# First stage of a hybrid encoder step: TensorE's queue written down in slots of one channel tile

## The chip, the cores and the metric

One core of a Trainium2 chip runs the whole step in one launch. The metric is the device time of that launch in microseconds; runs of one kernel are compared by their median. Engines are named as the profile names them: PE is TensorE, DVE is VectorE, ACT is ScalarE, POOL is GpSimd, and SP is SyncE, which issues every DMA of this kernel.

## What is computed

One layer takes 4096 tokens of a new stream (the prompt) and 32 tokens of a running one (the sample), 1024 wide:

```python
h    = rmsnorm(x, ln_pre)
proj = h @ w_in            # B_a | C_a | X_a | Z_a | qkv | Z_g | a_dec | b_beta
# group A: y_a = B_a * conv3(C_a * X_a) * silu(Z_a)                  (512 channels)
# group B: q, k, v = silu(conv4(qkv)); q, k L2-normalised            (4 heads of 128)
a_mat = strict_lower((kb * beta) @ kb.T) * decay
t_mat = triangular_solve(a_mat, eye, unit_diagonal=True)
u, w  = t_mat @ (v * beta), t_mat @ (k * beta * exp(g))
# chunk after chunk, with the state S handed on:
v_new = u - w @ S
o     = (q * exp(g)) @ S + attn @ v_new
S     = S * exp(g_last) + kdec.T @ v_new
y = x + rmsnorm(concat(y_a, rmsnorm(o) * silu(Z_g)) @ w_out, ln_post)
```

Each product of the big matrices is made of three products of float16 halves; the small products of group B are float32.

## The kernel before, in words

The program has two stages. **The first stage** makes group B: it projects q, k, v and Z_g and runs the gated recurrence. **The second stage** makes group A and the output product. Only the first is touched.

The prompt is cut into 16 blocks of 256 tokens, each with two chunks of 128 tokens. A block has 16 channel tiles of 128 columns of `w_in`, which `proj` takes in pairs: `qkv_pair` for k (two pairs), q (two) and v (two), `z_pair` for Z_g (two). One channel tile is 8 x 3 = 24 matmuls of 128x256 (lines 388 to 390, tiles `pj..`). The table `steps` (line 746) names the eight pairs in their order. Behind a pair, ACT copies the bank into `u`, ACT and DVE run the convolution (lines 403 and 405), and ACT the silu.

The rest of a block's group B is a chain of small groups of PE instructions with DVE, ACT or POOL work between them:

- `stage1(b, c)`, for each chunk: four transposes of k and of q (line 426, tile `gt`), then the gram products of k with k and q (line 442, `gq`), which DVE multiplies with the decay into `M` and `at` (lines 443 and 444).
- `subst(b)`: the 32x32 diagonal blocks of `M` go out to `lad` (line 450) and come back as `la` (line 485); DVE makes a factor `rl` (lines 488 to 490); POOL then runs a forward substitution, one multiply (line 495) and 31 pairs of a multiply and a subtract (lines 499 and 500), each waiting for the one before. The result goes out to `ltd` (line 503) and comes back in eight small DMAs as `Tc` (line 510).
- `merge(b)`: five groups of small PE instructions (lines 546, 551, 554, 557 and 560, tile `m`), with DVE or ACT between any two of them, build the inverse `U` out of `Tc` and `M`. DVE transposes `Tc` into `U` (line 531).
- `rec_a(b, c)`: transposes of v (`rt`), products with the state S (`rk`, `rq`, lines 580 and 585), with `U` (`rv`, line 591) and the update of S (`rS`, line 596). `rec_b(b, c)`: the product with `at` (`oo`), a norm on DVE and ACT, transposes (`om`, line 625) and the gate.

Around these stand `xprep` of the next block (norm of x, transposes by DMA), `gates` and `decays` of the next block (the tiles `ggate`, `gcs`, `gB`), and `prep_a`, which prepares the second stage's weights in 16 halves on DVE, ACT and POOL.

The main loop (line 767) runs over groups: group 0 holds the sample and block 0, group 1 block 1, and so on. Inside a group it emits the eight pairs, and between them the small groups: `finish(prevs, si)` for the block before in steps 0 to 3, `stage1` of this block in steps 4 and 5 (3 and 4 in the last `LS` = 2 groups). That is the order in which the code is written, not the order on the engines. The program is built with `schedule_with_timeline_sim=True`: a scheduler with its own costs of every instruction decides the order of each engine's queue, and on PE it places the small groups, often in pieces, between single matmuls of a channel tile. On the chip each engine works through its queue in that order and waits on semaphores.

PSUM tiles come from `bank`: `pj`, `g` and `r` have two buffers each, `o` and `m` one.

Of the kernel before, what the change touches and what calls it, by code (L numbers as in the profile page):

```python
# [18 lines left out]
P = 128  # L19
# [15 lines left out]
LS = 2  # L35
# [15 lines left out]
def hybrid_kernel(  # L51
# [7 lines left out]
    V, G, A, T = nc.vector, nc.gpsimd, nc.scalar, nc.tensor  # L59
# [107 lines left out]

    def scaled(cts, n=P, urow=None):


        ws = []
        first = cts[0] >= 16
        nm = f"{cts[0]}"
        L = bank("r" if first else "g", [P, 2, P], f"L{nm}")[:, :len(cts), :n]
        for i, ct in enumerate(cts):
# [10 lines left out]
            if not first:  # L186
                for kn in (4, 2, 1):
                    V.tensor_tensor(ab[:, 0:kn], ab[:, 0:kn], ab[:, kn:2 * kn], ALU.add)
            for k in range(kn):
                T.matmul(L[:, i], ones16, ab[:, k, :], start=k == 0, stop=k == kn - 1)  # L190
            ws.append(w)
        e = te([P, 2, P], I32, "we", 1, nm)[:, :len(cts), :n]
# [8 lines left out]
        for i, w in enumerate(ws):  # L201
            V.tensor_tensor(w, w, bc(e[:, i].bitcast(F32), 1, KT), ALU.mult)
        if urow is None:
# [4 lines left out]
        return ws  # L208
# [173 lines left out]
    def proj(b, cts, nm):  # L382
        n = b["n"]
        pt = bank("pj", [P, 2, NB1], f"{b['id']}_{nm}")
        for i, ct in enumerate(cts):
            wh, wl = W[ct]
            for k in range(KT):
                T.matmul(pt[:, i, :n], wh[:, k, :], b["hi"][:, k, :n], start=k == 0, stop=False)  # L388
                T.matmul(pt[:, i, :n], wh[:, k, :], b["lo"][:, k, :n], start=False, stop=False)  # L389
                T.matmul(pt[:, i, :n], wl[:, k, :], b["hi"][:, k, :n], start=False, stop=k == KT - 1)  # L390
        return pt

    def qkv_pair(b, c0, dst):

        n = b["n"]
        pt = proj(b, (16 + c0, 17 + c0), f"c{c0}")
# [11 lines left out]
    def z_pair(b, c0):  # L408
        n = b["n"]
        pt = proj(b, (28 + c0, 29 + c0), f"z{c0}")  # L410
# [4 lines left out]
    def stage1(b, c):  # L415
# [4 lines left out]
        ss = b["ss"]  # L420
        nm = f"{b['id']}_{c}"
        jk = te([P, P], BF16, "jk", 2, nm)
        for x in range(2):
            tp = bank("g", [P, NH, P], f"t{x}{nm}")
            for h in range(NH):
                T.transpose(tp[:C, h, :], qk[:, h, x, sl], ident)
            for h in range(NH):
                A.activation(jk[:C], tp[:C, h, :], AF.Square, accum_out=ss[:, c, x, h:h + 1])
            if x == 0:
                kd = (te if b["s"] else tl)([P, NH, P], F32, "hl" if b["s"] else "kd", 4, nm)[:C]  # L430
                V.tensor_tensor(kd, tp[:C], bc(b["ed"][:, c], 2, P), ALU.mult)
                b["kd"].append(kd)
# [15 lines left out]
        for q in range(C // 32):  # L448
            s = slice(32 * q, 32 * q + 32)
            dma(b["lad"][c, :, q].rearrange("h j i -> j h i"), M[s, :, s])  # L450

# [64 lines left out]
    def merge(b):  # L516
# [26 lines left out]
        for q in (0, 2):  # L543
# [3 lines left out]
            V.tensor_tensor(X[s1], px[s1], bc(nb_[s1], 3, 32), ALU.mult)  # L547
        for q in (0, 2):
# [3 lines left out]
            A.activation(U[s0, :, :, s1], pu[s0], AF.Copy)  # L552
        for c, h in ch:
            T.transpose(pt[:, c, h], U[0:64, c, h, 0:64], ident[:64, :64])
        A.activation(Y[0:64], pt, AF.Copy)
        for c, h in ch:
            T.matmul(py[:, c, h], M[c][0:64, h, 64:128], Y[0:64, c, h], start=True, stop=True)
        V.tensor_tensor(Y[64:128], py, bc(nb_[64:128], 3, 64), ALU.mult)
        for c, h in ch:
# [5 lines left out]
    def rec_a(b, c):  # L565
# [4 lines left out]
        qk, v, U, kd = b["qk"], b["v"], b["U"][c], b["kd"][c]  # L570
        S = state[b["s"]]
# [4 lines left out]
        for h in range(NH):  # L576
            A.activation(R[:, h], vt[:, h], AF.Copy, scale=b["br"][:, c, h:h + 1])
        pk = bank("r", [P, NH, P], f"k{nm}")[:C]
# [8 lines left out]
        for h in range(NH):  # L587
            A.activation(o[:, h], pq[:, h], AF.Copy, scale=b["e1"][:, c, h:h + 1])
        pv = bank("r", [P, NH, P], f"v{nm}")[:C]
# [3 lines left out]
        A.activation(vn, pv, AF.Copy)  # L593
        pS = bank("r", [P, NH, P], f"S{nm}")
# [6 lines left out]
        b["rec"] = (o, vn)  # L601

    def rec_b(b, c):
# [4 lines left out]
        o, vn = b["rec"]  # L608
# [13 lines left out]
        V.tensor_tensor(o, o, bc(f, 2, P), ALU.mult)  # L622
        pm = bank("o", [P, NH, P], f"m{nm}")[:, :, :C]
# [10 lines left out]
    def setup_block(b):  # L634
# [10 lines left out]
        b["kd"], b["M"], b["at"] = [], [], []  # L645

    def prep_b(ct):

        for i, w in enumerate(scaled((ct, ct + 1))):
# [6 lines left out]

    wa = {"next": 0}

    def prep_a():
# [7 lines left out]
        if not half:  # L667
            wa["w"] = scaled((ct, ct + 1))
# [70 lines left out]
    wgf, = scaled((32,), 8, ug)  # L739
# [8 lines left out]
    def finish(prevs, si):  # L748

        for p in prevs:  # L750
            n = p["nch"]
            if si == 0:
                merge(p)
            elif si == 1:
                rec_a(p, 0)
            elif si == 2:
                rec_b(p, 0)
                if n > 1:
                    rec_a(p, 1)
            elif si == 3:  # L760
                if n > 1:
                    rec_b(p, 1)
                if p["last"]:
                    out_state(p)

    prevs = []
    for gi, grp in enumerate(groups):
        for b in grp:
            setup_block(b)
            if b["s"]:  # L770
                b["hist"] = te([P, 12, 3], F32, "hists", 2, "i")
                if gi:
                    for c in range(0, 12, 2):
                        init_hist(b, 16 + c)
                state[1] = te([P, NH, P], F32, "hl", 4, "s0")
                dma(state[1], state_gdn[0, 0].rearrange("h k v -> k h v"))
            elif gi:
                b["hist"] = groups[gi - 1][-1]["hist_new"]
        for si, (kind, c0) in enumerate(steps):
            if gi == 0 and si == 4:  # L780
# [3 lines left out]
            if gi == 0:  # L784
                for kd_, c_ in steps[:si + 1 + (AH if si >= AS else 0)]:
                    ct = (28 if kd_ == "z" else 16) + c_
                    if ct not in W:
                        prep_b(ct)
                if kind != "z":
                    init_hist(smp, 16 + c0)  # L790
            for b in grp:
                n = b["n"]
                if kind == "z":
                    z_pair(b, c0)
                elif kind == "v":
                    qkv_pair(b, c0, b["v"][:, c0 - 8:c0 - 6, :n])
                else:
                    h0 = c0 % 4
                    qkv_pair(b, c0, b["qk"][:, h0:h0 + 2, 0 if kind == "k" else 1, :n])
            finish(prevs, si)  # L800
            if si == (2 if gi else 6) and gi + 1 < len(groups):
                for b in groups[gi + 1]:
                    xprep(b)
            s1 = 4 if gi + LS < len(groups) else 3
            if si in (s1, s1 + 1):
                for b in grp:
                    if si - s1 < b["nch"]:
                        stage1(b, si - s1)
            if si == s1 + 1:
# [3 lines left out]
            if si == (3 if gi else 7) and gi + 1 < len(groups):  # L813
                in_turn([gates(b) for b in groups[gi + 1]])
            if si == 6 and 1 <= gi <= 13 or si == 2 and gi in (4, 7, 10):

                p = grp[-1] if si == 6 else prevs[-1]
# [435 lines left out]
```

## Time and profile before

| | |
|---|---|
| Runs | 2394.66 us median of 3 (2390.61 to 2403.79) |
| The profiled execution | 2393.51 us, span 2391.8 us |
| PE busy | 2156.4 us, 90% of the span |
| PE weight loads | 1706.8 us, 71% |
| DVE busy | 1699.0 us, 71% |
| ACT busy | 992.5 us, 41% |
| POOL busy | 1195.2 us, 50% |
| Mean granted clock of PE | 0.962 |

The profiled execution lies 1.15 us below the median of the runs. The first stage reaches from the start to about 1320 us, the second from there to the end, with the recurrence of the last two blocks beside its beginning. The busy time of PE counts modelled ends of pipelined matmuls that overlap, so the distance from start to start is what a matmul costs. A number behind "<-" in a row names what ended an idle time of the engine.

### The profile page before, as it was taken

How to read it: one execution, taken by the hardware profiler on the slowest of the kernel's cores; microseconds unless marked ns; L12 is line 12 of the kernel's file. 1: busy time of each engine (PE TensorE's matmuls, PEld its weight loads, DVE VectorE, ACT ScalarE, POOL GpSimd, SP SyncE). 2: the span in 40 equal slices, each digit the busy share in tenths (PEclk: the TensorE clock that was granted, in tenths of full speed). 3: DMA queues.
4: the chain of work that ended last, by engine and by line, in shares of the span. 5: the costliest groups of instructions: out<-in, count | busy, mean ns of one | idle time of the engine just before them, and what ended most of it. 6: DMA issues, size and time to landing. Idle time of an engine off the chain costs nothing. (4 is left out here: it accounts for less than half of the span.)

```text
span 2391.8 us, 48652 instructions
## 1 busy us (share of the span) xinstructions
PE 2156.4 (90%) x18626; PEld 1706.8 (71%) x18626; DVE 1699.0 (71%) x4666; ACT 992.5 (41%) x2497; POOL 1195.2 (50%) x1581
## 2 busy tenths in 40 slices
PE   3677989899999999999999799899999999999998
PEld 3566877778777777787778678788888887444443
DVE  4886878987689888786777675676575565666763
ACT  4454656565666566555654220222121121433321
POOL 3526246752575644454454740766456611554542
PEclk9888999999999999999989899999999999999999
DMA  6334333534333442244324304311211133443431
GB/s 117 53 93 106 80 75 96 116 82 92 92 100 78 109 112 75 68 91 118 70 72 125 101 24 174 104 66 54 80 59 39 54 100 98 136 150 115 157 115 54
DMA packets 296913, 221.39 MB, mean 93 GB/s; under 512 B 166392, under 2 KB 236856, under 8 KB 296680
## 3 DMA queue, kind: packets, MB, share of 16 engines
q1 hardware_dynamic: 296680, 218.28, 33.5%
q8 instruction: 146, 2.39, 0.4%
q14 instruction: 87, 0.71, 0.1%
HBM read 127.84 MB, written 74.64 MB: 85 GB/s over the span
## 5 line engine op out<-in xcount | busy, mean ns | idle before, releaser
L388 PE MATMUL pj_c<-hhi,w 128*128 128x256 f16 x1536 | 429.3, 280 | 1.2 <-DMA hhi<-xth 1.2
L390 PE MATMUL pj_c<-hhi,w 128*128 128x256 f16 x1536 | 429.7, 280 | 0.0
L389 PE MATMUL pj_c<-hlo,w 128*128 128x256 f16 x1536 | 428.9, 279 | 0.0
L867 PEld LDWEIGHTS <-w_a 128*128 128x128 f16 x2880 | 269.9, 99 | 59.5 <-issue 25.6
L1130 PEld LDWEIGHTS <-opm 128*128 128x128 f16 x1536 | 149.6, 98 | 189.8 <-issue 15.5
L500 POOL TENSOR_TENSOR lt<-lt 128x112 f32<-128x112 f32 (+29 forms) x496 | 250.0, 504 | 38.9
L495 POOL TENSOR_TENSOR la<-la,lt 128x1024 f32<-128x1024 f32 x16 | 38.7, 2421 | 449.9 <-DVE lt L490 270.9
L390 PEld LDWEIGHTS <-w 128*128 128x128 f16 x2176 | 215.5, 100 | 53.2 <-POOL w L652 23.0
L499 POOL TENSOR_TENSOR lt<-la,lt 128x112 f32<-128x112 f32 (+29 forms) x496 | 233.1, 470 | 38.8
L388 PEld LDWEIGHTS <-w 128*128 128x128 f16 x2176 | 215.8, 100 | 34.1 <-issue 2.1
L389 PEld LDWEIGHTS <-w 128*128 128x128 f16 x2176 | 215.7, 100 | 30.7 <-issue 0.5
L405 DVE SCALAR_TENSOR_TENSOR qk<-u,cw,qk 128x256 f32<-128x256 f32 x384 | 214.9, 596 | 9.0 <-ACT qk L403 8.4
L867 PE MATMUL pja<-op,w_a 128*128 128x256 f16 x1536 | 194.5, 276 | 7.0 <-DVE w L881 3.4
L1079 POOL TENSOR_TENSOR mab<-mab 128x1024 bf16<-128x1024 bf16 (+2 forms) x48 | 103.6, 2159 | 130.8 <-ACT mab L1077 128.4
L867 PE MATMUL ga<-op,w_a 128*128 128x256 f16 x1152 | 149.8, 275 | 14.0 <-DVE w L881 8.1
L389 PE MATMUL pj_z<-hlo,w 128*128 128x256 f16 x512 | 144.6, 282 | 0.0
L390 PE MATMUL pj_z<-hhi,w 128*128 128x256 f16 x512 | 144.4, 282 | 0.0
L388 PE MATMUL pj_z<-hhi,w 128*128 128x256 f16 x512 | 144.3, 282 | 0.0
L1130 PE MATMUL pjo<-w_o,opm 128*128 128x512 f16 x528 | 118.2, 379 | 3.8 <-DVE v13y L1154 2.0
L1130 PE MATMUL ro<-w_o,opm 128*128 128x512 f16 x504 | 114.7, 383 | 3.9 <-DVE v7y L1154 2.0
L881 DVE TENSOR_TENSOR w<-pja,w 128x256 f32<-128x256 f32 x168 | 67.4, 420 | 70.6 <-PE pja L867 68.0
L1130 PE MATMUL go<-w_o,opm 128*128 128x512 f16 x504 | 112.7, 379 | 3.9 <-DVE v19y L1154 2.0
(707 smaller groups left out, 4946.5 us busy)
## 6 DMA issues: line engine op xcount, KB each, us to landing
xt<-in_x_prompt_dram SPq DMA_DIRECT2D x32, 512.0 KB
op<-hTd SPq DMA_DIRECT2D x32, 512.0 KB
mx<-mxd SPq DMA_DIRECT2D x16, 1024.0 KB
xtw<-in_w_in_dram SPq DMA_DIRECT2D x28, 512.0 KB
wad<-hl SPq DMA_DIRECT2D x56, 256.0 KB
gB<-gd SPq DMA_DIRECT2D x16, 516.0 KB
hTd<-hhi SPq DMA_DIRECT2D x16, 512.0 KB
hTd<-hlo SPq DMA_DIRECT2D x16, 512.0 KB
```

What stands on the lines that cost most here:

```text
L388: T.matmul(pt[:, i, :n], wh[:, k, :], b["hi"][:, k, :n], start=k == 0, stop=False)
L389: T.matmul(pt[:, i, :n], wh[:, k, :], b["lo"][:, k, :n], start=False, stop=False)
L390: T.matmul(pt[:, i, :n], wl[:, k, :], b["hi"][:, k, :n], start=False, stop=k == KT - 1)
L405: V.scalar_tensor_tensor(d, u[:, i, j:j + n], cw[:, j, c0 + i:c0 + i + 1], d, ALU.mult, ALU.add)
L495: E.tensor_tensor(la, la, bc(rl, 1, 32), ALU.mult)
L499: E.tensor_tensor(tm, bc(la[:, j, j + 1:32], 2, w), bc(lt[:, j, 0:w], 1, r), ALU.mult)
L500: last = E.tensor_tensor(lt[:, j + 1:32, 0:w], lt[:, j + 1:32, 0:w], tm, ALU.subtract)
L867: T.matmul(out, lt(x, k), rh(y, k), start=start and k == n == 0, stop=stop and k == 3 and n == 2)
L881: V.tensor_tensor(dst, p, src, ALU.add)
L1079: G.tensor_tensor(ab[:, 0:m], ab[:, 0:m], ab[:, m:2 * m], ALU.add)
L1130: T.matmul(p, mo[:, x, k, t * P:t * P + m], WO[y, k][:, hf * 512:hf * 512 + 512], start=k == i == 0, stop=k == KT - 1 and i == 2)
```

## The change

PE's order in the first stage no longer comes from the scheduler. A wrapper `Ordered` stands in for `nc.tensor`: from group 1 to the end of the first stage it ties every PE instruction to the one written before it, without a semaphore. The other engines' queues are still made by the scheduler, around that fixed order.

The code is therefore written in the order that PE is to have. The unit is a slot, one channel tile of 24 matmuls; a block has 16 of them, and slot number s0 + i is the i-th one from the start of block b's own group (s0 = 16 x group). `at_slot` files a function under a slot, `run_slot` calls the functions of a slot behind its channel tile. The functions with PE work in several parts became generators (`qkv_pair`, `z_pair`, `merge`, `rec_a`, `rec_b`, `scaled`, `prep_a`), so that each part can be filed by itself; `stage1` is split into `norm_qk` and `gram`. `LS` is gone: the last blocks are treated as the others. In `scaled`, for the second stage's weights, the last of three additions writes to a tile of its own and the bank `L` is taken later.

```diff
-    V, G, A, T = nc.vector, nc.gpsimd, nc.scalar, nc.tensor
+    V, G, A = nc.vector, nc.gpsimd, nc.scalar
+    class Ordered:
+        on = False
+        last = None
+        def queue(self, i):
+            ins = getattr(i, "ins", i)
+            if self.on and self.last is not None:
+                tc.add_manual_dep(ins, self.last.name, mybir.DependencyInfo(
+                    mybir.DependencyClass.NoSync, mybir.DependencyReason.DATA), reason="order")
+            self.last = ins
+            return i
...
+    T = Ordered()
...
-    def finish(prevs, si):
...
+    def finish(p, s0):
...
+        at_slot(s0 + 22, next, ra[0])
+        at_slot(s0 + 23, next, ra[0])
+        for i in range(5):
+            at_slot(s0 + 24 + i, next, mg, None)
+        at_slot(s0 + 29, next, ra[0])
+        at_slot(s0 + 30, ends, ra[0])
+        at_slot(s0 + 30, next, rb[0])
+        at_slot(s0 + 28, next, ra[1])
+        at_slot(s0 + 32, next, ra[1])
+        at_slot(s0 + 34, next, ra[1])
+        at_slot(s0 + 34, ends, rb[0])
+        at_slot(s0 + 35, ends, ra[1])
+        at_slot(s0 + 35, next, rb[1])
+        at_slot(s0 + 39, ends, rb[1])
...
+            T.on = True
...
+            at_slot(s0 + 7, norm_qk, b, 0, 0)
+            at_slot(s0 + 8, norm_qk, b, 1, 0)
+            at_slot(s0 + 10, norm_qk, b, 0, 1)
+            at_slot(s0 + 11, gram, b, 0)
+            at_slot(s0 + 11, norm_qk, b, 1, 1)
+            at_slot(s0 + 12, gram, b, 1)
+            at_slot(s0 + 12, rnorms, b)
+            at_slot(s0 + 12, subst, b)
+            if gi + 1 < len(groups):
+                nx = groups[gi + 1][0]
+                g = gates(nx)
+                at_slot(s0 + 2, xprep, nx)
+                at_slot(s0 + 9, next, g)
+                at_slot(s0 + 10, next, g)
+                at_slot(s0 + 13, ends, g)
+            finish(b, s0)
+            for si, (kind, c0) in enumerate(steps):
+                ps = pair(b, kind, c0)
+                next(ps)
+                run_slot(s0 + 2 * si)
+                ends(ps)
+                run_slot(s0 + 2 * si + 1)
...
+                        with tc.issue_after(p["subst_end"]):
+                            pa = prep_a()
+                            if next(pa, 0) is None:
+                                at_slot(s0 + 11, next, pa)
+                                at_slot(s0 + 13, ends, pa)
...
+    T.on = False
```

Two places in the built order show what moves. The first is PE where the merge of block 8 begins, during the channel tiles of block 9. `pj9_..` is a bank of that block's projection, `m8` the merge's bank, `Tc8` the substitution's result. Before:

```order
L388 LDWEIGHTS w20_26_1454
L388 MATMUL pj9_c10_11530<-hhi9_10167,w20_26_1454 128x256
L546 MATMUL m8_10906<-Tc8_10676,M8_0_10462 32x32
L389 LDWEIGHTS w20_26_1454
L389 MATMUL pj9_c10_11530<-hlo9_10168,w20_26_1454 128x256
L546 MATMUL m8_10906<-Tc8_10676,M8_0_10462 32x32
L390 LDWEIGHTS w21_26_1455
L390 MATMUL pj9_c10_11530<-hhi9_10167,w21_26_1455 128x256
```

With the change (the wrapper's lines 74 and 77 stand for all matmuls and transposes):

```order
L74 LDWEIGHTS w17_24_1209
L74 MATMUL pj9_c8_11197<-hhi9_9848,w17_24_1209 128x256
L74 MATMUL m8_11227<-Tc8_10596,M8_0_10411 32x32 x4
L74 MATMUL m8_11227<-Tc8_10596,M8_1_10481 32x32 x4
L74 MATMUL m8_11227<-Tc8_10596,M8_0_10411 32x32 x4
L74 MATMUL m8_11227<-Tc8_10596,M8_1_10481 32x32 x4
L77 MATMUL gt09_1_11247<-ident_63,qk9_10776 128x128 x4
L74 LDWEIGHTS w18_25_1212
```

The merge's first group was spread over the matmuls of a channel tile, one piece between a few of them; it now stands in one piece behind the tile of slot 8.

The second place is DVE where it takes up `Tc7`, the substitution's result of block 7 (`o6`, `zg6`: the output of block 6; `kd8`, `u8`, `v8`: stage 1 and convolution of block 8; `u9`: of block 9). Before:

```order
L621 TENSOR_TENSOR so6_1_9217<-so6_1_9217,sm6_8457 128x4
L398 COPY u9_6_11019<-hist8_9784 128x2x3
L531 STREAM_TRANSPOSE U_144<-Tc7_9625 32x8x32 x2
L622 TENSOR_TENSOR o6_1_9062<-o6_1_9062,so6_1_9217 128x512
L531 STREAM_TRANSPOSE U_144<-Tc7_9625 32x8x32 x2
L547 TENSOR_TENSOR Rx7_9853<-m7_9854,sm7_9540 32x256
L431 TENSOR_TENSOR kd8_1_10550<-gt08_1_10541,E38_9313 128x512
```

With the change:

```order
L471 TENSOR_TENSOR kd8_0_10124<-gt08_0_10115,E38_9602 128x512
L429 COPY u8_10_10389<-hist7_8640 128x2x3
L583 STREAM_TRANSPOSE U_144<-Tc7_9538 32x8x32 x4
L599 TENSOR_TENSOR Rx7_10187<-m7_10188,sm7_9453 32x256 x2
L471 TENSOR_TENSOR kd8_1_10217<-gt08_1_10208,E38_9602 128x512
L431 COPY hist8_9725<-u8_8_10243 128x6
L436 SCALAR_TENSOR_TENSOR v8_9723<-u8_8_10243,cw_98,v8_9723 128x256 x3
```

Before, block 7's `Tc` was taken up after the next block's first gram and beside the output of block 6; now before that gram, with the convolution of v of block 8 behind it in the queue.

## Rows read from the trace of the kernel before

**Rows 1.** Busy time by engine in one stretch, with granted clock and DMA:

```profile
core 0: us, PE busy (x) PEld busy (x) DVE busy (x) ACT busy (x) POOL busy (x), PEclk, DMA share, GB/s
300.00:1300.00 1000.00, 923.16 (x8568) 782.44 (x8569) 798.60 (x2442) 576.97 (x1570) 548.67 (x1019) 0.96 0.38 91
```

**Rows 2.** Waits of PE, 444 to 1055 us (total us, times, longest):

```profile
PE m L546 <- DMA Tc<-ltd: 12.7, 9, 2.4
PE rk L580 <- DVE S L599: 8.2, 8, 3.0
```

**Rows 3.** PE in time (start, length, [idle before]): merges of blocks 0, 8, 9, 10, 15:

```profile
241.66 0.24 PE L546 MATMUL m<-Tc,M 32*32 32x32 f32 x2
...
830.78 0.24 PE L546 MATMUL m<-Tc,M 32*32 32x32 f32 x2 [1.43 <-DMA Tc<-ltd]
...
911.32 0.24 PE L546 MATMUL m<-Tc,M 32*32 32x32 f32 x2 [1.98 <-DMA Tc<-ltd]
...
991.64 0.24 PE L546 MATMUL m<-Tc,M 32*32 32x32 f32 x2 [1.75 <-DMA Tc<-ltd]
...
1370.91 0.31 PE L546 MATMUL m<-Tc,M 32*32 32x32 f32 x2 [6.09 <-DMA Tc<-ltd]
```

**Rows 4.** PE in order of time: last gram products of blocks 9 and 10:

```profile
857.70 1.03 PE L442 MATMUL gq<-qk 128*128 128x256 f32 x4
...
939.03 1.03 PE L442 MATMUL gq<-qk 128*128 128x256 f32 x4
```

**Rows 5.** Block 9 from gram to merge: DVE, SP and POOL in order of time:

```profile
858.76 0.42 DVE L443 TENSOR_TENSOR M<-gq,gB 128x256 f32<-128x256 f32 x1
...
859.22 1.73 SPq L450 DMA_DIRECT2D lad<-M  x4
...
863.73 1.71 SPq L485 DMA_DIRECT2D la<-lad  x4
...
867.81 0.19 DVE L488 TENSOR_SCALAR lt<-la 128x32 f32<-128x32 f32 x1 [0.76 <-DMA la<-lad]
...
868.69 2.36 POOL L495 TENSOR_TENSOR la<-la,lt 128x1024 f32<-128x1024 f32 x1 [23.74 <-DVE xss L115]
...
907.34 0.20 POOL L500 TENSOR_TENSOR lt<-lt 128x8 f32<-128x8 f32 x1
...
909.30 4.28 SPq L510 DMA_DIRECT2D Tc<-ltd  x8
```

**Rows 6.** PE in order of time: what groups cost from start to start:

```profile
707.28 1.16 PE L585 MATMUL rq<-S,qk 128*128 128x128 f32 x8
708.28 1.03 PE L442 MATMUL gq<-qk 128*128 128x256 f32 x4
709.24 0.69 PE L551 MATMUL m<-U,Rx 32*32 32x32 f32 x16
709.86 0.28 PE L388 MATMUL pj_c<-hhi,w 128*128 128x256 f16 x1
...
712.38 1.03 PE L442 MATMUL gq<-qk 128*128 128x256 f32 x4
```

**Rows 7.** Busy time and granted clock behind one merge:

```profile
911.70:921.90 10.20, 9.52 (x51) 5.76 (x51) 10.16 (x20) 4.28 (x12) 8.66 (x11) 0.50 0.37 87
```

**Rows 8.** PE in order of time: the last projection matmul of the first stage:

```profile
1320.27 0.27 PE L390 MATMUL pj_z<-hhi,w 128*128 128x256 f16 x1
```

**Rows 9.** DVE by line, 444 to 1055 us (busy, mean ns); four steps at 915.86:

```profile
L405 DVE SCALAR_TENSOR_TENSOR v<-u,cw,v 128x256 f32<-128x256 f32 x96 | 46.1, 517 | 0.9 <-ACT v L403 0.6
...
L531 DVE STREAM_TRANSPOSE U<-Tc 32x256 f32<-32x256 f32 x32 | 13.9, 435 | 13.1 <-DMA gd<-row 6.7 <-DMA Tc<-ltd 6.0
...
915.86 4.59 DVE L405 SCALAR_TENSOR_TENSOR v<-u,cw,v 128x256 f32<-128x256 f32 x4
```

**Rows 10.** Busy time during the substitutions of blocks 9 and 13:

```profile
868.70:907.50 38.80, 34.27 (x326) 30.60 (x325) 35.44 (x97) 22.45 (x54) 33.94 (x63) 1.00 0.50 103
1187.60:1221.20 33.60, 33.60 (x330) 30.94 (x328) 28.01 (x77) 16.91 (x59) 28.74 (x64) 1.00 0.13 43
```

More of the change, by code (lines that the diff above doesn't have):

```diff
@@ L202, in scaled @@
             V.tensor_tensor(w, w, bc(e[:, i].bitcast(F32), 1, KT), ALU.mult)
+        if not first:
+            yield
         if urow is None:
@@ L667, in prep_a @@
         if not half:
-            wa["w"] = scaled((ct, ct + 1))
+            yield from scaled((ct, ct + 1))
             return
@@ L746, in hybrid_kernel, with at_slot, run_slot, ends @@
     steps = [("k", 4), ("k", 6), ("q", 0), ("q", 2), ("v", 8), ("v", 10), ("z", 0), ("z", 2)]
-    def finish(prevs, si):
[L750 to L767, printed above, removed]
+    slots = {}
+    def at_slot(i, fn, *a):
+        slots.setdefault(i, []).append(lambda: fn(*a))
+    def run_slot(i):
+        for fn in slots.pop(i, ()):
+            fn()
+    def ends(gen):
+        for _ in gen:
+            pass
+    def finish(p, s0):
+        n = p["nch"]
+        ra = [rec_a(p, c) for c in range(n)]
+        rb = [rec_b(p, c) for c in range(n)]
+        mg = merge(p)
+        if n == 1:
+            for i, g in enumerate((ra[0], ra[0], mg, ra[0], ra[0], rb[0])):
+                at_slot(s0 + 16 + i, next, g, None)
+            at_slot(s0 + 24, ends, rb[0])
+            at_slot(s0 + 24, out_state, p)
+            return
+        at_slot(s0 + 22, next, ra[0])
[12 more added lines that the diff above has]
+        at_slot(s0 + 39, ends, rb[1])
+        if p["last"]:
+            at_slot(s0 + 36, out_state, p)
+    def first_group(grp):
         for b in grp:
@@ L783, in hybrid_kernel @@
                     decays(b)
[L784 to L790, printed above, removed]
-            for b in grp:
[L792 to L805, printed above, removed]
+            for kd_, c_ in steps[:si + 1 + (AH if si >= AS else 0)]:
+                ct = (28 if kd_ == "z" else 16) + c_
+                if ct not in W:
+                    prep_b(ct)
+            if kind != "z":
+                init_hist(smp, 16 + c0)
+            for b in grp:
+                ends(pair(b, kind, c0))
+            if si == 6:
+                xprep(groups[1][0])
+            if si in (4, 5):
                 for b in grp:
-                    if si - s1 < b["nch"]:
-                        stage1(b, si - s1)
-            if si == s1 + 1:
+                    if si - 4 < b["nch"]:
+                        stage1(b, si - 4)
+            if si == 5:
                 for b in grp:
@@ L826, in hybrid_kernel @@
         prevs = grp
-    while wa["next"] < 16:
-        prep_a()
+    T.on = False
     early.close()
-    for si in range(4):
-        finish(prevs, si)
+    for i in sorted(slots):
+        run_slot(i)
     late.close()
```

149 lines of the change are left out of this document (95 added, 54 removed).

## The prediction

> **What bounds the kernel now.** I read the table of stretches first. From 300 to 1300 us PE is busy 923 of 1000 us, DVE 799, POOL 549, at a mean clock of 0.96 [rows 1]: PE seems to be the bound of the first stage, with little idle time. The waits of PE come next. Over eight blocks the longest is for `Tc`, the substitution's result (12.7 us), then for the state S (8.2) [rows 2]. A queue written by hand could win those few microseconds per block. But which waits are left depends on what PE's queue may put in front of the substitution, so the third view is a block's loop, in order of time.
>
> The merge of block 0 begins at 241.66 us, that of block 15 at 1370.91 [rows 3]: 1129.25 us for 15 blocks, **75.3 us a block**. Two stretches make up a block's loop.
>
> *From the last gram product to the merge.* Block 9's gram ends on PE at 857.70 + 1.03 = 858.73 [rows 4], its merge begins at 911.32 [rows 3]: 52.6 us. Hardly any of it is PE's [rows 5]: DVE has M at 859.18, SP issues `lad` and, when that has landed, `la`; DVE waits for `la` until 867.81; POOL substitutes from 868.69 to 907.54, 38.85 us; `ltd` goes out, `Tc` is issued from 909.30 on, and the first merge instruction starts 2.0 us behind that. Block 10's stretch is 991.64 - 940.06 = 51.6 us [rows 3, 4]. PE waited 1.98 and 1.75 us at the end of these two [rows 3], so it is this chain, not PE, that ended them.
>
> *From the merge to the next block's last gram product.* 858.73 - 830.78 = 27.95 us for block 8, 940.06 - 911.32 = 28.74 us for block 9 [rows 3, 4].
>
> **The change, part by part.** *The loop.* The table puts the second gram in slot 12 and the merge in slot 24, for every block. So PE has 12 channel tiles, ten groups of four f32 products, four groups of transposes and the gates' small products to put under the first stretch. A tile is 24 x 0.11 = 2.63 us (23 matmuls from 709.86 to 712.38), a group of f32 products 1.0 us (707.28 to 708.28) [rows 6]; transposes are put at 0.5 and the gates at 1, estimates from those groups. 31.6 + 10 + 2 + 1 = **44.6 us of PE for a chain of 52.1** (mean of 52.6 and 51.6). PE must stop in slot 24 for up to 7.5 us, less what it loses to other waits on the way, and nothing in its queue may go ahead. Before, the scheduler hid that: in the built order there stand between gram and merge 9.8 to 13.7 tiles, as it suited, and the merge's first pieces lie between single matmuls.
>
> The second stretch has four tiles in the table (10.5 us), five parts of the merge (0.6 us for each of two [rows 6], 1 for the others, an estimate), four halves of gram at 0.96 [rows 6], three groups of transposes and the gates: some 21 us. I don't take 21 but what such a stretch took. The merges of blocks 8, 9 and 10 are the places of the kernel before that look most like the table: 11.8 to 12 tiles in the first stretch and 4.2 to 4.3 in the second, by the built order. Their loops took 80.5 and 80.3 us [rows 3], and the blocks in which the scheduler pulled the next gram up to the merge made up for it. The table has no such blocks. So the loop is 52.1 + 28.3 = **80.4 us for every block**, against 75.3.
>
> Two terms could move the 28.3. In pieces the merge pays for the change of tile size each time, which goes; and `Tc` comes in eight copies issued over 4.28 us [rows 5], a time that PE filled with matmuls and now spends waiting. Neither has a row of its own in the new order: between nothing and 4.3 us, and I take nothing, since the rows with the likeliest order already hold both. The other term is the clock. [...]
>
> *The waits that the table takes away* [rows 2] lie under the first stretch or in the second's 28.3; under the first they are worth nothing while the chain has 7.5 us to spare.
>
> *Moved without cost.* `xprep` three slots earlier, `gates` to slots 9 to 13 and `prep_a` behind slot 7 keep their instructions and DMAs. On SP, what is filed ahead of `ltd` waits for nothing later than slot 3 in the built order; on POOL, `prep_a` has the 41 us between two substitutions; on DVE, the factor for the substitution no longer stands behind the next block's decay, but `la` arrived later than that at block 9 [rows 5]. The new tile and later bank in `scaled` add no instruction.
>
> *Beginning and end.* Group 0 isn't tied, so the merge of block 0 stays at 241.66: its substitution sets it. The merge of block 14 comes at 241.66 + 14 x 80.4 = 1367.3; the last gram 28.3 later; three tiles (7.9) and three f32 groups (3.0) then end the projection at 1406.5, where it now ends at 1320.54 [rows 8]: **+86.0 us**. The second stage starts then. The merge of block 15 follows 41.3 us behind the projection's end, where now it is 50.4, and the 6.09 us that PE waits for it [rows 3] should go: **-6**. In one formula, the change is 14 x loop - 1045.8 us, here +79.8. On the profiled execution's 2393.5 us (1.2 below the median) that makes **2473 us**.
>
> **The rivals.** *The DVE queue stands too* (slower still). In the new order DVE's transposes of `Tc` have a convolution, the gates and the gram's products behind them. Four transposes are 1.7 us, a convolution step is 0.52 us but 1.15 while POOL works on `prep_a` (four in 4.59) [rows 9]. If DVE falls behind and the 4.3 us of `Tc` landing are added whole, the loop is 84.7: 14 x 84.7 - 1045.8 = +140, **2534 us**. For it: DVE was busy all 10.2 us behind that merge [rows 7]. Against: blocks 8 and 9 had this load too.
>
> [...]
>
> *The substitution gets shorter* (faster). The same 63 POOL instructions took 38.8 us beside 35.4 us of DVE work and 33.6 beside 28.0 [rows 10]. If DVE's work moves out of that stretch, the chain is 52.1 - 5.2 = 46.9 us, about what PE has to do with its small waits; then PE hardly stops, the clock stays up, and the loop is 46.9 + 23.2 = 70.1: -64, **2329 us**. It decides where the loop falls under 74. [...] Against it: the built order puts about as many DVE instructions between the factor and the transposes of `Tc` as before, 107 to 115 against 107 to 129.
>
> That the order is not taken over is no rival: the built queue shows the merge in one piece.
>
> **How the numbers follow.** Forecast 0.54 (loop 77 to 83, 2426 to 2510), DVE standing 0.13, clock up 0.11, substitution shorter 0.22. The range leaves out most of the last case and the end of the second: 2355 to 2535. About 0.5%, 12 us, is what a measurement can tell from no change. Faster by more 0.22, within 0.11, slower by more 0.67.
>
> **What would show it.** Right: merges some 80 us apart from block 1 to 15; PE's wait for `Tc` at the merge grown from 1 to 2 us to 4 to 7 in every block and the longest in the list, while the waits for S, R and the gates shrink; a lower granted clock behind each merge; PE busy under 90% from 300 to 1300. Wrong: merges 70 us apart with PE waiting under 2 us there; or POOL's substitution under 35 us; or a last projection before 1320 us.

## The result, and the profile after

The changed kernel takes 2538.39 us (median of 4 runs, 2534.81 to 2541.04) against 2394.26: ratio **1.0595**, 95% interval 1.056 to 1.0629. The profiled execution took 2536.03 us, 142.5 more than that of before. The forecast was slower, by 79.8 us; the median lies 3 us above the range.

The stretch that answers to [rows 1]:

```profile
core 0: us, PE busy (x) PEld busy (x) DVE busy (x) ACT busy (x) POOL busy (x), PEclk, DMA share, GB/s
300.00:1300.00 1000.00, 844.14 (x7690) 730.41 (x7691) 716.74 (x2196) 532.65 (x1405) 461.15 (x871) 0.90 0.34 84
```

PE is busy for 79 us less of the same 1000, and its mean clock is 0.90 for 0.96: less idle was the aim of a written queue, and there is more. The merges and last grams (PE in order of time; [rows 3, 4] answer to them):

```profile
245.51 0.69 PE L74 MATMUL m<-Tc,M 32*32 32x32 f32 x16
...
512.11 0.69 PE L74 MATMUL m<-Tc,M 32*32 32x32 f32 x16
...
535.43 1.89 PE L74 MATMUL gq<-qk 128*128 128x256 f32 x8
...
588.15 0.56 PE L74 MATMUL m<-Tc,M 32*32 32x32 f32 x12
...
930.90 0.69 PE L74 MATMUL m<-Tc,M 32*32 32x32 f32 x16
...
954.95 1.89 PE L74 MATMUL gq<-qk 128*128 128x256 f32 x8
...
1021.08 0.69 PE L74 MATMUL m<-Tc,M 32*32 32x32 f32 x16
...
1044.40 1.89 PE L74 MATMUL gq<-qk 128*128 128x256 f32 x8
...
1097.03 0.68 PE L74 MATMUL m<-Tc,M 32*32 32x32 f32 x8
...
1429.60 0.95 PE L74 MATMUL m<-Tc,M 32*32 32x32 f32 x8 [7.37 <-DMA Tc<-ltd]
...
1470.06 0.27 PE L74 MATMUL pj_z<-hhi,w 128*128 128x256 f16 x1
...
1517.58 0.31 PE L74 MATMUL m<-Tc,M 32*32 32x32 f32 x2 [6.75 <-DMA Tc<-ltd]
```

The merge of block 14 stands at 1429.60: (1429.60 - 241.66) / 14 = 84.85 us a block, and the prediction's formula with it, 14 x 84.85 - 1045.8, gives +142.1. The loops are not alike, though: 90.2 us from block 8 to 9, 75.9 from block 9 to 10. Over all 15 they go 76, 91, 99.5, 76, 88, 92, 75.5, 87, 90, 76, 88, 79, 85, 80, 88, with a period of three up to block 10, which is the period of the weights' preparation (`prep_a`) in the blocks. What PE waits for, over the eight blocks from the merge of block 3 to that of block 11 (total us, times, longest):

```profile
PE om L77 <- DVE o L682: 29.2, 5, 11.8
PE oo L74 <- DVE zg L688: 27.6, 8, 4.6
PE m L74 <- DVE Rx L599: 16.2, 8, 4.4
PE rS L74 <- ACT vn L652: 12.4, 8, 2.3
...
PE m L74 <- DMA Tc<-ltd: 3.3, 4, 1.8
```

`Tc`, the longest of [rows 2], has nearly gone. In its place stand waits for DVE: for the normed output `o`, for the gate `zg` that must be read out of the one bank `o` before the next `oo` may be written, and for `Rx` between the first two parts of the merge. One of the two longest is found in the loop to block 9. SP, DVE and PE there, in order of time:

```profile
991.76 0.53 SPq L299 DMA_DIRECT2D hTd<-hhi  x1
992.39 1.68 SPq L205 DMA_DIRECT2D xtw<-in_w_in_dram  x2
994.12 5.95 SPq L299 DMA_DIRECT2D hTd<-hlo  x1
1000.11 1.00 SPq L266 DMA_DIRECT2D xt<-in_x_prompt_dram  x1
1001.21 0.57 SPq L555 DMA_DIRECT2D ltd<-lt  x1
...
1009.09 4.22 SPq L562 DMA_DIRECT2D Tc<-ltd  x8
```

```profile
995.73 0.31 DVE L138 SCALAR_TENSOR_TENSOR so<-so 128x4 f32<-128x4 f32 x1
1004.62 1.22 DVE L206 TENSOR_TENSOR xtw<-xtw,lnp 128x1024 f32<-128x1024 f32 x1 [8.58 <-DMA xtw<-in_w_in_dram]
...
1013.39 0.68 DVE L682 TENSOR_TENSOR o<-o,so 128x512 f32<-128x512 f32 x1
```

```profile
1014.22 1.09 PE L77 MATMUL om<-ident,o 128*128 128x128 f32 x4 [11.69 <-DVE o L682]
```

The load of the weights (`xtw`) is issued at 992.39, among the transfers of `xprep` (the three other rows ahead of `ltd`). DVE's queue has the multiply of these weights in the middle of the norm of `o` (line 138 before it, line 682 behind), so DVE stands for 8.58 us, `o` is late, and PE, whose queue is fixed, stands for 11.69 us at `om`. The same rows show a second delay: `ltd` goes out at 1001.21, `Tc` not before 1009.09. From 300 to 1300 us DVE waits 45.3 us for such loads; before the change there is no such wait:

```profile
DVE xtw L206 <- DMA xtw<-in_w_in_dram: 45.3, 8, 9.0
```

### The profile page after: what moved, and what is told of

Same layout as the page of the kernel before. It is cut to its first block, busy times and chain, and to the rows that moved or that the text cites. A ratio compares the mean times of both kernels' runs of the same rounds, so it can differ in the third digit from the quotient of the medians.

```text
span 2534.2 us, 48623 instructions
## 1 busy us (share of the span) xinstructions
PE 2178.5 (86%) x18626; PEld 1745.3 (69%) x18626; DVE 1697.0 (67%) x4666; ACT 1003.4 (40%) x2497; POOL 1168.1 (46%) x1581
## 5 line engine op out<-in xcount | busy, mean ns | idle before, releaser
L74 PE MATMUL pj_c<-hhi,w 128*128 128x256 f16 x3072 | 583.3, 290 | 0.0
L74 PE MATMUL pj_c<-hlo,w 128*128 128x256 f16 x1536 | 445.4, 290 | 0.0
L552 POOL TENSOR_TENSOR lt<-lt 128x112 f32<-128x112 f32 (+29 forms) x496 | 237.5, 479 | 38.7
L551 POOL TENSOR_TENSOR lt<-la,lt 128x112 f32<-128x112 f32 (+29 forms) x496 | 219.0, 442 | 38.9
L436 DVE SCALAR_TENSOR_TENSOR qk<-u,cw,qk 128x256 f32<-128x256 f32 x384 | 208.4, 587 | 4.8 <-ACT qk L434 4.8
L74 PE MATMUL pj_z<-hhi,w 128*128 128x256 f16 x1024 | 180.3, 275 | 0.0
L1003 ACT ACTIVATE op<-tsc 128x512 f16<-128x512 f32 x60 | 37.8, 630 | 192.9 <-POOL tsc L1009 113.0
L468 ACT ACTIVATE jk<-gt 128x128 bf16<-128x128 f32 x256 | 71.0, 278 | 100.8 <-PE gt L77 95.2
L988 DVE TENSOR_TENSOR w<-ga,w 128x256 f32<-128x256 f32 x121 | 51.0, 422 | 77.6 <-PE ga L74 69.8
L436 DVE SCALAR_TENSOR_TENSOR v<-u,cw,v 128x256 f32<-128x256 f32 x192 | 84.6, 477 | 9.0 <-ACT v L434 9.0
```

What stands on the lines that cost most here:

```text
L74: return self.queue(nc.tensor.matmul(*a, **k))
L436: V.scalar_tensor_tensor(d, u[:, i, j:j + n], cw[:, j, c0 + i:c0 + i + 1], d, ALU.mult, ALU.add)
L468: A.activation(jk[:C], tp[:C, h, :], AF.Square, accum_out=b["ss"][:, c, x, h:h + 1])
L551: E.tensor_tensor(tm, bc(la[:, j, j + 1:32], 2, w), bc(lt[:, j, 0:w], 1, r), ALU.mult)
L552: last = E.tensor_tensor(lt[:, j + 1:32, 0:w], lt[:, j + 1:32, 0:w], tm, ALU.subtract)
L988: V.tensor_tensor(dst, p, src, ALU.add)
```

## The experiments

Each is an edit of the changed kernel; `...` stands for lines left out. As a measure of a loop I take the eleven from the merge of block 1 to that of block 12: 834.0 / 11 = 75.8 us before the change and 942.2 / 11 = 85.7 after it.

### Which part of the change costs: the fixed queue, or the places

**e1_free**: the code is in the new order, PE's queue the scheduler's.

```diff
-            T.on = True
+            T.on = False
```

> The wrapper stays off, so the code is written in the new order but PE's queue is again the scheduler's. Theory Q (PE's fixed queue stands behind DVE, and DVE behind the weights' load and POOL's weight work): the fixed queue is what costs, the time falls back to 2390 to 2425 us, PE's waits for o and zg fall from 93 us to under 25, and DVE may go on waiting 30 us or more for the load. Rival P (the new places of xprep, gates and the weights cost by themselves, whatever PE's order): 2480 to 2540 us.

2456.38 us, ratio 1.026 (1.0229 to 1.029): between the two. The fixed queue costs some 82 us, and the new places, with a free queue, are 62 us slower than the kernel before. DVE waits 50.0 us for the weights' load here too (nine waits), and PE's wait for `o` is hardly smaller, 44.8 us for 49.1 from 300 to 1300 us. What the free queue takes away there are the waits for `zg` (40.8 to 9.1), `Rx` (29.1 to 8.2) and `vn` (16.6 to 4.6).

**e8_free_tie**: e1_free, and the multiply is kept behind the gate `zg` in DVE's queue:

```diff
+    def tie(i, j): tc.add_manual_dep(getattr(i, "ins", i), getattr(j, "ins", j).name, mybir.DependencyInfo(mybir.DependencyClass.NoSync, mybir.DependencyReason.DATA), reason="order")
...
-            (V if ct in VLN or not first else G).tensor_tensor(w, w, bc(lnp, 2, n), ALU.mult)
+            m = (V if ct in VLN or not first else G).tensor_tensor(w, w, bc(lnp, 2, n), ALU.mult)
+            if "gate" in wa: tie(m, wa["gate"])
...
-        V.scalar_tensor_tensor(mg, pm, gwc, mg, ALU.mult, ALU.mult)
+        wa["gate"] = V.scalar_tensor_tensor(mg, pm, gwc, mg, ALU.mult, ALU.mult)
```

> On e1_free (2456 us, PE's queue left to the scheduler): DVE's multiply of the weights is tied behind the gate as in e2_tie. Theory W (of the 62 us that e1_free is above the kernel before, most is DVE standing on the weights' load, 50 us there, since the change dropped the tie to stage 1's end): PE's waits for o fall from 49 to under 15 us, 2395 to 2420 us. Rival (the other new places, xprep and gates, cost it): 2440 to 2460 us.

2425.44 us, 1.0131 (1.0104 to 1.0159): half of the 62 us are gone, and the time lies between the two theories.

**e10_free_prep** and **e11_free_old**: e1_free, the preparation back behind pair 6 with both its old ties; in e11 also `xprep` behind slot 5 and the gates behind slot 7.

```diff
-                if si == 3:
-                    for _ in range((1 <= gi <= 13) + (gi in (4, 7, 10))):
-                        p = prevs[-1]
-                        with tc.issue_after(p["subst_end"]):
+                if si == 6 and gi <= 13 or si == 2 and gi in (4, 7, 10):
+                        p = b if si == 6 else prevs[-1]
+                        with tc.issue_after(p["stage1_end"]), tc.issue_after(p["subst_end"]):
                             pa = prep_a()
...
+                            ends(pa)
```

> e1_free (2456 us) with the weights' preparation in its old place (behind pair 6, in three groups also behind pair 2) and with its old ties behind stage 1 and the substitution. Theory W (DVE stands behind the weights' load because the change filed it close to its use and dropped the tie): DVE's wait for the load goes from 50 to under 5 us, 2395 to 2425 us. Rival (xprep and gates): 2440 to 2460.

> e10_free_prep with xprep back behind slot 5 and the gates behind slot 7 as well. What then differs from the kernel before is where stage 1 and the steps of the recurrence are written, with PE's queue free. Theory O (these places cost nothing as long as PE's queue is free): 2385 to 2405 us. Rival: they cost too, 2415 us or more.

2446.75 us (1.0188 to 1.0252 of before) and 2419.38 (1.0081 to 1.0134). The old place alone gave back 10 us, against theory W, though DVE no longer waits for the load there; PE's wait for `Tc` at the merge takes its place (5.5 us in e1, 31.5 here). With `xprep` and the gates it is 37 us. The rest, 25 us, is left for what else the change moves, above all the places of stage 1 and the recurrence, even with a free queue; it was not split further.

### Moving single pieces under the fixed queue

**e2_tie**: the tie of e8, with PE's queue fixed.

> DVE's multiply of the weights stands behind the gate of the older block's second chunk. Theory Q alone: PE's waits for o (49 us, 11.7 to 17.6 in blocks 2, 5, 8) go, and with them 42 us in the three long loops, 8 us in the others and some clock: about 2485 us. Rival C (behind it the chain over Tc comes next: in these three loops Tc is issued 12 us late, 52 to 57 us behind the gram): only 5.7 to 6.2 us in each of the three loops and up to 1.5 in four others, 2512 to 2520 us, and PE's wait for Tc grows by 5 us in each of the three. If DVE's wait for the load has nothing to do with it: 2538.

2543.72 us, 1.0632 (1.0593 to 1.0671): nothing is gained. The waits for `o` are gone from the list. The stretches from gram to merge in the loops to blocks 3, 6 and 9 fall, from 69.8, 64.1 and 64.2 us to 58.5, 53.5 and 54.3, but those from merge to gram grow, from 29.1 to 33.9 us in the mean. The loops are 86.3 us, nearly alike from block 3 on (84.8 to 88.0); these are PE's waits from block 1 to 12:

```profile
PE m L74 <- DVE Rx L599: 37.7, 11, 5.2
PE oo L74 <- DVE zg L688: 33.6, 11, 3.4
PE m L74 <- DMA Tc<-ltd: 31.9, 52, 8.3
```

PE now comes to the merge ahead of `Tc` in most blocks. It waits for its pieces, then for `Rx`, because DVE's transposes of `Tc` start as late.

**e3_load**: `preload` takes the weights' two tiles and files their loads at the group's start; `scaled` then uses these tiles.

```diff
...
-            setup_block(b)
+            setup_block(b); preload(gi)
```

> The weights' loads are filed at the start of the group, ahead of xprep. Theory Q: DVE no longer waits for them (45 us in eight waits fall to under 5), the waits for o go, and if it was these loads that delayed the substitution's result through DRAM, Tc is issued 45 to 48 us behind the gram in blocks 3, 6 and 9 too (now 52 to 57): loops of 76 to 80 there, about 2485 us. Rival D (the result is late because of xprep's transfers): Tc stays 52 us or later and the time is 2510 to 2520. Rival B (the buffers that the loads now hold make xprep late): slower than 2538.

2608.32 us, 1.0915: rival B by the time. PE waits 38.5 us at the gates for `hhi` and `hlo` (25.3 + 13.2), the results of `xprep`. But the loads were not early on the chip: SP issues them in the same place as in the changed kernel, among the transfers of `xprep` (954.26 for a multiply at 965.61), DVE still waits 41.9 us for them, and PE's longest wait is again for `o`, 81.5 us. So this run says nothing on what an earlier load would be worth. `Tc` is still issued 46 to 60 us behind the gram.

**e4_sub**: the substitution leaves out every second step.

```diff
-        for j in range(31):
+        for j in range(0, 31, 2):
```

> The substitution leaves out every second of its 31 steps (the inverse's diagonal blocks are not those of the reference). POOL's 35 us fall to about 18. Rival C (as predicted: the chain from gram over POOL and Tc to the merge ends every block's loop): every loop falls, those of 76 us to about 70, and the time to 2440 to 2470 us. Theory Q: the chain ends the loop only in the four loops of 76 us (3 to 5 us each to be had, until PE's own work ends it), the others are set by PE's waits behind DVE; with some 10 us at the last two merges: 2500 to 2525 us.

2512.6 us, 1.0501 (1.0471 to 1.0532), by the number theory Q. But the loops from block 1 to 12 stay at 86.2 us; what is won lies at the end. `Tc` is issued more than 20 us before the merge there, and PE's wait for `o` grows to 84.9 us in eleven blocks.

**e5_oo**:

```diff
-        at_slot(s0 + 35, next, rb[1])
-        at_slot(s0 + 39, ends, rb[1])
+        at_slot(s0 + 36, next, rb[1])
+        at_slot(s0 + 40, ends, rb[1])
```

> Alone against the changed kernel (2538 us): the second output product of a block (oo, then om) stands one slot later. [...] Theory C (the first stretch is ended by the chain over Tc, so what PE waits for inside it is covered): PE's wait for Tc grows by what is won, 2515 to 2540 us.

2553.61 us, 1.0668 (1.0639 to 1.0698), worse. The wait for `zg` went; 52.9 us of waits at `rq` for ACT's R, up to 13.5, came.

**e6_m1**, **e7_m2**: merge and followers one or two slots later, on e2_tie. The preparation goes along, two and four slots, and in e7 the second `oo` stands three later. From e7:

```diff
...
-            at_slot(s0 + 24 + i, next, mg, None)
+            at_slot(s0 + 26 + i, next, mg, None)
...
```

> On e2_tie (2544 us): the merge and what follows it stand one slot later, so that 13 channel tiles lie between gram and merge and three between merge and gram; the weights' preparation follows two slots later. Theory C alone: the first stretch stays at 51.5 us, the second loses one tile: 14 x 2.6 = 37 us, 2507 us, with a wait for Tc of 1 to 5 us left. [...]

> On e2_tie (2544 us): merge and followers two slots later, the second output product three, the weights' preparation four. Theory C alone: 2 x 37 us less, 2470 us. [...]

2493.57 us (1.0388 to 1.0449) and 2544.22 (1.06 to 1.0654). One slot, with the preparation two later, is worth 50 us. At two, PE waits 61.0 us at `ggate` for `kd`: DVE's queue has its transposes of `Tc` ahead of that `kd` and stands there.

**e12_m2_u**: e7 with these transposes tied behind the last `kd`.

```diff
...
-            V.transpose(Uf[s, :, s], Tf[s])
+            i = V.transpose(Uf[s, :, s], Tf[s]); T.on and tie(i, wa["kd"])
```

> e7_m2 (2544 us) with DVE's transposes of Tc tied behind the kd of the running block, the one that PE's gates wait for (70 us in 12 waits there, up to 13 us: DVE stood at the transposes, waiting for Tc, with kd behind them). Theory S (a fixed queue on PE turns the order of DVE's queue into PE's waits): the waits for kd fall under 15 us, with the clock behind them 6 to 9 us a block: 2420 to 2460 us. Theory C: the wait moves to Tc at the merge, 2500 us or more. Under 2394 us would make it faster than the kernel before.

2523.79 us, 1.054 (1.0516 to 1.0565). The wait for `kd` halves, to 29.1 us, and that for `Rx` doubles, from 25.5 to 51.7. Each of these moves takes one wait away and makes another.

### Two causes side by side

e9, e13, e14 and e15 take away the weights' preparation, the chain over `Tc`, or both.

**e9_tie_sub**: e2_tie with every second step of the substitution left out.

> e2_tie (2544 us) with every second step of the substitution left out (the inverse's diagonal blocks are not those of the reference). In e2_tie all loops are alike, 51.5 us from gram to merge, which is the chain, and 34.4 from merge to gram. Theory C (the chain ends the loop, and the wait for Tc at its end is what brings the clock down): Tc lands at 38 us, PE no longer waits at the merge, the first stretch is PE's own 47 to 50 us and the second 25: loops of 72 to 77 us, and with 10 to 15 us at the last two merges 2370 to 2420 us. Rival R (the second stretch is long because DVE is late with Rx and the clock falls behind that, whenever Tc comes): the first stretch as above, the second still 32 us or more: loops of 80 us and over, 2460 us or more.

2492.19 us, 1.0419 (1.04 to 1.0439): rival R by the time, both theories by the loops. From block 1 to 12, four loops take 74 to 76 us, as theory C has it; those in which the weights are loaded or scaled take 88 to 96, though the last piece of `Tc` is issued by 38 us behind the gram. DVE waits 27.9 us for the loads there, the tie notwithstanding.

**e13_late**: the 16 halves of the preparation behind the first stage.

```diff
-                    for _ in range((1 <= gi <= 13) + (gi in (4, 7, 10))):
+                    for _ in range(0):
...
     T.on = False
+    while wa["next"] < 16: ends(prep_a())
```

> The changed kernel with all 16 halves of the weights' preparation written behind the first stage; to be read by the loops of blocks 1 to 11, which then hold none of it, not by the whole time. Theory W (the table as such takes 76 us a block, and what it loses comes from the weights' preparation on DVE, POOL and SP): every loop 75 to 78 us, where the changed kernel has 75.5 to 99.5. Theory C/K as predicted (PE is early for Tc in every block, and pays the clock each time): 79 us or more. The whole time is expected above 2420, since the preparation then stands before the second stage.

**e14_late_m1**: the same, merge and followers one slot later.

> e13_late with the merge and its followers one slot later. If the chain from gram to merge ends these loops, each falls by one channel tile, 2.6 us, to about 73; if PE's own work and its small waits end them, they stay within 1 us; if Rx and o become late again as in e6_m1, they grow to 79 to 82.

**e15_late_sub**: e13 with every second step of the substitution left out.

> e13_late with every second step of the substitution left out as in e4_sub. With neither the weights nor the chain over Tc, what is left is PE's own work and its waits for DVE and ACT inside the block: theory W says 72 to 74 us a loop (the chain was worth 2 to 4 us), theory C 68 to 71.

The whole times of the three are 2682.65, 2611.67 and 2561.24 us (1.1185, 1.0903, 1.0681), since the preparation now stands before the second stage. The loops tell more. The stretches from block 1's merge to block 12's of the kernel before, of the changed one, and of e13, e14, e15:

```profile
327.00:1161.00 834.00, 771.61 (x7205) 654.50 (x7205) 674.63 (x2064) 488.86 (x1300) 459.08 (x825) 0.96 0.39 93
```

```profile
321.60:1263.80 942.20, 793.30 (x7248) 688.14 (x7247) 675.84 (x2076) 500.75 (x1318) 435.21 (x825) 0.90 0.34 83
```

```profile
312.80:1217.60 904.80, 792.23 (x7206) 685.00 (x7205) 609.84 (x1970) 461.09 (x1255) 335.05 (x748) 0.92 0.27 64
```

```profile
311.20:1157.50 846.30, 760.29 (x7206) 665.58 (x7205) 600.53 (x1970) 461.42 (x1254) 336.21 (x748) 0.94 0.28 68
```

```profile
295.30:1123.60 828.30, 763.14 (x7207) 665.03 (x7206) 568.97 (x1970) 461.51 (x1255) 188.28 (x418) 0.96 0.29 70
```

Without the preparation the loops of e13 are alike: 904.8 / 11 = **82.3 us**. Theory W falls; this is the prediction's case. One of them on PE:

```profile
640.26 0.52 PE L74 MATMUL m<-Tc,M 32*32 32x32 f32 x8
...
669.00 1.89 PE L74 MATMUL gq<-qk 128*128 128x256 f32 x8
...
723.10 0.57 PE L74 MATMUL m<-Tc,M 32*32 32x32 f32 x6 [0.46 <-DMA Tc<-ltd]
```

30.6 us from merge to gram, 52.2 from gram to merge. Its waits from block 1 to 12:

```profile
PE oo L74 <- DVE zg L688: 35.3, 11, 3.4
PE m L74 <- DVE Rx L599: 23.8, 11, 2.3
PE rS L74 <- ACT vn L652: 22.5, 11, 2.3
PE m L74 <- DMA Tc<-ltd: 15.2, 45, 1.4
```

With half the substitution left out as well, e15, the loop is 828.3 / 11 = 75.3; with one slot more between gram and merge, e14, it is 846.3 / 11 = 76.9, 5.3 us less for one tile of 2.6. So for the loop: both causes 85.7, the chain alone 82.3, the weights alone 84.7 (e9, (1255.7 - 324.0) / 11) or 86.2 (e4), neither 75.3. **Either alone leaves most of the loss**, and taking one away shows little.

Two things have to be said of "the chain alone". In e13 the chain is not only the substitution: in each of these blocks SP's queue has `mxd<-zg` between `ltd` and `Tc`, and it waits for DVE's gate (the last section has the rows). `Tc` is issued 4.5 us behind `ltd` in the mean, where `ltd` alone needs 1.7 to 1.8. In e14 it is 1.7 us, in e15 2.5. And e15 also frees DVE: the same 1970 instructions take 569.0 us beside the shorter substitution for 609.8. But e14, with POOL as busy as in e13, gives nearly the same loop as e15, so PE's late `Tc`, and not POOL's load, makes most of the difference. How much of it is SP's order was not tried alone.

The 75.3 are over both theories' numbers for e15, nearer theory W's: PE's waits for `zg` and `vn` are still there, 19.8 and 15.3 us in eleven blocks.

No version tried beats the kernel before; e11_free_old comes nearest. The table's loop of 75.3 us, without the preparation and half the substitution, is about what that kernel takes with both.

## Why the prediction was right or wrong

*The form of the sum held.* The change is 14 x loop - 1045.8: +142.1 for a measured 142.5. Behind the projection's end, 1470.33 us, come 1063.9 us to the end of the span, where before they were 1071.3: -7.4 for the -6 of the text.

*The loop was mis-sized*: the formula's 80.4 comes out as 84.85, and 14 x 4.45 = 62 us is the whole miss. 4 us of it are merge 0, which came at 245.51 for 241.66: it stands where the table puts it, `Tc` being issued at 223.42, and not where its substitution ends, as the text had it. The other 58 us lie in the 14 loops, with means of 55.3 us from gram to merge and 29.3 from merge to gram; the text had 52.1 and 28.3.

*The step that failed* is "Moved without cost": `prep_a` behind slot 7. In the loops to blocks 3, 6 and 9 the stretch from gram to merge is 69.8, 64.1 and 64.2 us, together 42 more than 3 x 52.1; that is nearly all of the 14 x 3.2 = 45 by which it exceeds. There PE stood at `om` behind DVE, and DVE behind the load. Without the preparation, e13, a loop is 3.4 us shorter, 37 us in the eleven loops from block 1 to 12, which exceed 80.4 by 58 in all. I followed `prep_a` on POOL and looked on SP for what is filed ahead of `ltd`, but never asked how long its load needs. Before, the load at 346.6 us had 57 us until its multiply at 403.7, and the code had a tie that held that multiply behind stage 1's end; the change drops this tie and files the load next to its use, 992.39 for 1004.62 in block 9's loop. That it is the lost lead time that costs, and not the preparation's work as such, the rows say for the three long loops; no run gave the lead time back under the fixed queue. With a free queue it was worth 10 of 62 us (e10), and a tie on the multiply alone 31 (e8).

*The first stretch, 52.1.* Outside these three loops it is 52.4 us in the mean, but the reason was wrong, so this is luck. The text let the chain over POOL and `Tc` end it, with PE standing. In block 4 the gram ends at 537.32, `Tc` is issued at 583.08, 45.8 us behind it, and PE begins the merge at 588.15 without a wait. These 50.8 us are PE's own, with its waits for `vn`, `zg` and others on the way; the text had 44.6 us of work there. In e15, where `Tc` is issued 17 us or more before the merge, it is 49.9; in e13, 51.8, and PE waits at most 0.5 us for the first piece.

*The second stretch, 28.3.* Here the late `Tc` costs. From e13 to e15 the loop falls by 7 us, 5.1 of them here (30.5 to 25.4): in e13 PE waits 1.4 us a block for the pieces of `Tc` and 2.2 for `Rx`, whose transposes start as late, and behind that the matmuls of the next tile start 0.21 us apart (648.03 to 649.74 us), for 0.11 ahead of the merge. Behind block 4's merge, at 559.08, the granted clock is 0.50 from 562 to 568 us, with the same 0.21. The late `Tc` is the term that the text put "between nothing and 4.3 us" and took as nothing. The price of the merge's pieces, which it put there too, can be read from the kernel before: with two 32x32 matmuls between them, two 128x256 ones start 0.38 us apart and not 0.11 (992.15 and 992.53 us), and with the change 16 in one piece are busy for 0.69. In the changed kernel the second stretch is 25.2 us behind the three long first stretches, where `Tc` had landed, and 30.2 to 34.1 behind the merges of blocks 1, 4, 7 and 10.

*PE's wait for `Tc`, 4 to 7 us in every block*, was 3.3 us in eight blocks. The spare 7.5 us that I left PE under the first stretch went to waits that the table itself makes, for `vn` and `zg`, 1.3 + 2.9 us in a good block, and the clock behind them (0.55 in the rows below); in the long loops `om` took more than that.

*The clock.* I let it fall once a loop, behind the merge. Behind the waits for `vn` and `zg` it was low as well:

```profile
988.00:994.00 6.00, 6.00 (x32) 4.77 (x33) 4.93 (x12) 3.98 (x12) 5.17 (x11) 0.55 0.97 220
```

These six us are PE's first behind its wait of 2.94 us at `oo`, which came 1.2 us after one of 1.17 us for `vn`; it is busy throughout, at a mean clock of 0.55. Up to 993.4 us the granted clock is 0.50 and one matmul follows another after 0.21 us, from 993.5 on it is 1.00 and they follow after 0.11. Not every wait at a merge is followed by this: in the kernel before the clock was 1.00 for ten us behind the merge of block 6 (700.2 to 710.2 us), where PE had waited 1.25 us, and 0.50 behind that of block 9 [rows 7], after 1.98 us. What the low clock is worth can be read from the stretches above: for nearly the same work PE is busy 793.3 us in the changed kernel and 771.6 before. So 21.7 of the 108.2 us are longer busy time, which goes with the mean clock of 0.90 for 0.96, and 86.5 are idle time. In e13 against e15 it is 29.1 of 76.5.

*The rivals.* "The DVE queue stands too" named 2534 us, nearly the time, by another mechanism: `Tc`'s landing of 4.3 us in every block. Its kind is there, `Rx` at 16.2 us in eight blocks, but 2 us a block isn't what was missing, and the three long loops are another matter. "The substitution gets shorter" came half true: block 9's takes 34.1 us, under the 35 that I gave as the sign of a faster kernel, against 38.85 [rows 5]. DVE is busy 27.1 of the 34.2 us there, fewer than in [rows 10]. In block 9 the chain did not shorten with it, since `Tc` came 7.9 us behind `ltd`. In block 4 it did (34.9 us, and 45.8 us from gram to `Tc` for 50.6 in block 9 before), and PE came later than `Tc`; but the loop was 76.0 us and not 70.1, since PE's own way takes 50.8. That sign was badly chosen. A clock that stays up, 0.11, was rightly held unlikely: its mean was 0.90, for 0.96 before. The 23.2 us that the loop of 70.1 has for the second stretch no run shows: behind the changed kernel's merges of blocks 8 and 9, where the clock was 1.00 throughout, the second stretch took 25.9 and 25.2 us. Slower, with a chance of 0.67, was right, and a range up to 2535 was too short at the side on which several small waits add up.

## What to carry to other kernels

Here a queue written by hand turned the lateness of other engines into waits of this one (for `zg` 40.8 us from 300 to 1300 us, and 9.1 with a free queue): before fixing one, list for every group which instruction of another engine it needs, what stands ahead of that one in its own queue, and above all which DMA that queue itself waits for. When a piece of work is moved, count the lead time of its loads as well as its instructions. And where two chains end a loop side by side, experiments that remove one show little; remove both, and then put each back alone. Where a scheduler makes the other queues, read them in each such run before comparing two: e13 and e14 differ in SP's order too.

## What the runs showed of the hardware

How long one small transfer took to land differed with what was still moving when it was issued: 1.7 us in one block, 7.9 in another. It is the substitution's result, 128 KB (`ltd`); `Tc` may be issued when it has landed. In the changed kernel's block 4 four transfers of 512 KB go out 8.3 to 5.9 us ahead of `ltd`:

```profile
573.08 0.55 SPq L299 DMA_DIRECT2D hTd<-hhi  x1
573.73 1.72 SPq L266 DMA_DIRECT2D xt<-in_x_prompt_dram  x2
575.50 0.52 SPq L299 DMA_DIRECT2D hTd<-hlo  x1
581.36 0.33 SPq L555 DMA_DIRECT2D ltd<-lt  x1
...
583.08 4.34 SPq L562 DMA_DIRECT2D Tc<-ltd  x8
```

From `ltd` to `Tc` it is 1.7 us, as before the change (907.57 to 909.30 in block 9). In block 9 of the changed kernel, behind five of 512 KB in 9.5 us, the last of them 1.1 us ahead, it is 7.9. The same two stretches by what moves:

```profile
581.40:583.10 1.70, 1.70 (x18) 1.57 (x16) 1.27 (x2) 0.85 (x3) 1.70 (x2) 1.00 0.23 77
1001.20:1009.10 7.90, 1.33 (x13) 0.95 (x10) 4.37 (x12) 2.88 (x7) 1.99 (x2) 0.87 0.68 218
```

77 GB/s over 1.7 us are 131 KB, about `ltd` itself; 218 over 7.9 us are 1.7 MB. The prediction set the price of `xprep` and of the loads in the chain at nothing; in blocks 3, 6 and 9 it is 6 to 10 us (`Tc` 11.5, 8.2 and 7.9 us behind `ltd`). The long wait at `om` hid it there; in e2, without that wait, PE stood 8.3, 3.5 and 3.8 us at these merges.

A late issue can look the same. DVE, POOL and SP in e13, block 6, in order of time for each engine:

```profile
717.84 0.75 DVE L688 SCALAR_TENSOR_TENSOR zg<-om,gwc,zg 128x512 f32<-128x512 f32 x1 [1.67 <-PE om L77]
```

```profile
715.83 0.32 POOL L543 MEMSET lt<- 128x256 f32 x1 [1.82 <-DMA ltd<-lt]
```

```profile
714.04 0.32 SPq L555 DMA_DIRECT2D ltd<-lt  x1
718.62 0.37 SPq L693 DMA_DIRECT2D mxd<-zg  x1
719.03 5.62 SPq L562 DMA_DIRECT2D Tc<-ltd  x8
```

`Tc` is issued 5.0 us behind `ltd`, but `ltd` had landed after 1.8: that is when POOL, which waits for it, goes on. SP's queue has `mxd<-zg` ahead of `Tc`, and that waits until DVE's gate ends at 718.59, behind PE's own `om` of the slot before the merge. So in e13 3 of the 5 us are the order of SP's queue. In the changed kernel that order costs time in one block only, block 13, where `Tc` is issued 5.0 us behind `ltd`.
